# The v stage and the u seam of a hybrid decoder block: shorter roots, diagonals on ScalarE, another order of operands

## The chip, the cores and the metric

The kernel runs on one core of a Trainium2 chip. The metric is the device time of one execution in microseconds (us). TensorE (PE) multiplies, VectorE (DVE) and ScalarE (ACT) do the elementwise work, each in the order of its own queue, and SyncE (SP) issues nearly all DMAs. TensorE's clock is granted by a throttle at one of two levels, 1.2 and 2.4 GHz.

## The reference, cut to what matters

```python
h = rms_norm(x, norm_mix_g[l])                       # x: 1024 tokens x 1024
proj = h @ w_in[l]
rnn_x, rnn_gate, sgu_u, sgu_v, gate_a, gate_b = jnp.split(proj, SPLIT_POINTS, axis=-1)
rnn_x = causal_depthwise_conv(rnn_x, conv_w[l], conv_b[l])
y_a = jax.nn.gelu(rnn_gate) * rg_lru(rnn_x, ..., rg_lambda[l])
y_b = chunked_sgu(jax.nn.gelu(sgu_u), jax.nn.gelu(sgu_v), ...)
# chunked_sgu: v = layer_norm(v); in chunks of 128 tokens mixed = tril(w_s) @ v + b_s; u * mixed
merged = sigmoid(gate_a) * (y_a @ w_proj_a[l]) + sigmoid(gate_b) * (y_b @ w_proj_b[l])
x = x + merged @ w_out[l]
x = x + swiglu(rms_norm(x, norm_ffn_g[l]))           # d_ff 2816
return rms_norm(x, norm_final_g)
# in rg_lru: log_a = -8 * r * softplus(-rg_lambda)
```

## The kernel before

Every matrix product is made of three passes in reduced fp32: an operand is kept as a high part and a low part, and high by high, high by low and low by high are summed (`mm3`, L96 to L99). `split` (L92 to L94) makes the parts: ACT copies the high part, DVE subtracts it for the low one. Most projections are Strassen-Winograd products of 2 x 2 blocks (`wino`, L231): seven products M1 to M7 of blocks and sums of blocks (A11, A12, A22 and the sums S1 to S4 of the activations; b11 to b22 and the sums t1 to t4 of the weights), each with 4 x 3 matmuls of 128 x 512. The weight parts of a product are made by `weight` and `pump` when the product is written, or `state["ahead"]` products earlier.

The program starts with the v stage (pool `phv`, L458 to L785). Its order on each engine is that of the code. x comes in transposed in four blocks (`xt_load`), is scaled and split (`x_split`), and multiplied with the two halves of the v weights, wv0 and wv1, in eight tiles of 128 tokens each (`pv0`, `pv1`). 1/rms of the tokens (`x_rms`) is computed from x in rows by `rstd_early`, a Newton iteration on DVE on one or two columns, and is spread over the free axis by a matmul of ones with a diagonal matrix (`x_diag`, tiles `dg`). A LayerNorm over v (`v_stats`, `v_norm`, `v_centre`; roots for two tiles at once where possible) gives `vn` (`v_split`), which `v_mix` multiplies with the causal 128 x 128 mix weights into PSUM tiles `mx`; ACT and DVE add their two parts into `mt` (`v_mixed`), and SP stores these to the DRAM buffers `mix_d`. Between the tiles of pv1 the operands A11, S1 to S3 and so on are computed from the scaled x (`part`, `sums`, `sum_s4`), because PE needs them right behind.

Then the two u projections, `u0` and `u1`, run product by product in the order M1, M2, M5, M6, M3, M7, M4, with the last two mixes between them (the seam, L752 to L785). Their results wait in PSUM (`postponed`), and `take(n)` takes n of them out. At the end of the seam the pool `phv` is closed and `phr` opened in its place, where `u_out` (L835) loads the mix from `mix_d`, applies the LayerNorm scale and shift (L847), the gelu (L848) and the product (L850) and stores the branch. The recurrence's constants (softplus of lambda, tiles `sp_*`, L873 to L891) and copies of A22 (L866) stand there too. From r0 on, pairs of r, u and g projections follow, then the output projections, the SwiGLU and the last norm, none of which the change edits.

ACT's functions are kept in tables; a function of another table costs an `ACT_TABLE_LOAD` on ACT.

Of the kernel before, what the change touches and what calls it, by code (L numbers as in the profile page):

```python
# [28 lines left out]
RG_C = 8.0  # L29

# [21 lines left out]
def block_kernel(ctx: ExitStack, tc: tile.TileContext, a: dict, out: bass.AP):  # L52
# [323 lines left out]
    act.activation(small.tile([P, 1], F32, name="warm", bufs=1), eps_t, AF.Gelu_apprx_tanh)  # L376
# [16 lines left out]
    def rstd_early(pool_, var, scale, name, n=1, y=None):  # L393
# [5 lines left out]
        dve.tensor_scalar(h, var, -0.5 * scale, -0.5 * EPS, ALU.mult, ALU.add)  # L399
        dve.tensor_scalar(y.bitcast(I32), h.bitcast(I32), -0.5, float(0x5F3759DF - 2 ** 22 - 2 ** 30),  # L400
                          ALU.mult, ALU.add)
        for _ in range(3):
# [5 lines left out]
            dve.scalar_tensor_tensor(y, t, 1.5, y, ALU.add, ALU.mult)  # L408
# [49 lines left out]
    with tc.tile_pool(name="phv", bufs=1) as wk:  # L458
# [88 lines left out]
        def sums(i):  # L547
            s1 = s1s[i] = wk.tile([P, 2, HALF], F32, name=f"xs{i}", tag="shift")
            dve.tensor_add(s1, block(1, 0, i), block(1, 1, i))
            dve.tensor_sub(block(1, 0, i), block(0, 0, i), block(1, 0, i))  # L550
            dve.tensor_sub(block(0, 0, i), s1, block(0, 0, i))
# [13 lines left out]
        ms.__enter__()  # L565
        act.dma_start(pv, a["pv"])
# [10 lines left out]
        state["load"] = 2  # L577
        xt_load(1)
# [7 lines left out]
        for k in range(NK):  # L586
            pump(k + 1)
            x_split(0, (k,))
        acc = {t: ps(f"pv0{t}") for t in range(2)}

        warm = ps("warm")
        for _ in range(8):
# [885 lines left out]
```

## Time and profile before

| | us |
|---|---|
| median of 3 runs (1416.86 to 1420.11) | 1417.53 |
| the profiled execution, whole | 1417.34 |
| its span on the core | 1415.5 |
| PE busy in the span | 1396.2 (99%) |
| DVE busy | 1100.9 (78%) |
| ACT busy | 792.6 (56%) |

The span is the time from the first to the last recorded instruction of the core. PE's busy time counts a matmul at either clock alike, and successive matmuls overlap, so a loss is also looked for in the distance from one start to the next. Times in the rows are counted from the span's start.

### The profile page before, as it was taken

The numbers are of one execution on the slowest core, as the hardware profiler recorded it, in microseconds if no ns is written. First come the engines' busy times: TensorE is split into PE (matmuls) and PEld (weight loads), VectorE is DVE, ScalarE is ACT, GpSimd is POOL, SyncE is SP. The second block draws the span as 40 slices with busy tenths as digits, with TensorE's granted clock in tenths as the row PEclk, the third lists the DMA queues.
The fourth block names the chain that finished last, engine by engine and source line by source line (L and its number), as shares of the span: only waits on it lengthen the run. The fifth ranks groups of instructions, "written<-read, shape, count | busy, mean of one in ns | idle before, by whom it ended". The sixth has DMA issues, their size and how long they took to land.

```text
span 1415.5 us, 17195 instructions
## 1 busy us (share of the span) xinstructions
PE 1396.2 (99%) x6220; PEld 1152.2 (81%) x6220; DVE 1100.9 (78%) x1807; ACT 792.6 (56%) x1318; POOL 75.0 (5%) x59
## 2 busy tenths in 40 slices
PE   9998999999999999999999999999999999999997
PEld 7887887788788888888888788888888888888886
DVE  6999999988888879798756976666666664697586
ACT  8467688888889865443443543333333333444464
POOL 0000000000000000000000021111111111000000
PEclk9999999999999999999999999999999999999999
DMA  9323645433332388774611132232232226842342
GB/s 320 142 60 118 206 153 178 167 113 116 115 110 103 105 306 318 259 297 149 223 60 45 75 112 112 112 112 100 94 112 112 112 84 259 338 179 93 112 142 82
DMA packets 70566, 212.46 MB, mean 150 GB/s; under 512 B 6352, under 2 KB 20176, under 8 KB 57936
## 3 DMA queue, kind: packets, MB, share of 16 engines
q1 hardware_dynamic: 70192, 211.05, 41.7%
q8 instruction: 49, 0.80, 0.2%
q10 hardware_dynamic: 288, 0.30, 0.1%
q14 instruction: 37, 0.30, 0.1%
HBM read 148.68 MB, written 62.65 MB: 149 GB/s over the span
## 4 chain that ended last, share of the span: by engine, by line
PE 76%; DVE 12%; ACT 8%; issue 2%; DMA 1%; SPq 0%; DVEq 0%; ACTq 0%
PE f_p L97 10%; PE f_p L99 10%; PE f_p L98 10%; PE d_M L98 5%; PE d_M L99 5%; PE d_M L97 5%; PE g_p L99 2%; PE g_p L98 2%; PE g_p L97 2%; PE pa_p L99 2%; PE pa_p L98 2%; PE pb_p L99 2%; PE pb_p L98 2%; PE pa_p L97 2%; PE pb_p L97 2%
## 5 line engine op out<-in xcount | busy, mean ns | idle before, releaser
L93 ACT ACTIVATE dl_M<-wraw 128x512 fp32r<-128x512 f32 x77 | 48.6, 631 | 104.2 <-PE d_M L99 94.3
L93 ACT ACTIVATE f_t<-wraw 128x512 fp32r<-128x512 f32 x88 | 55.2, 630 | 84.3 <-PE f_p L99 64.1
L98 PE MATMUL d_M<-d_M,dl_M 128*128 128x512 f32 x260 | 101.2, 389 | 0.0
L97 PE MATMUL d_M<-d_M,dl_M 128*128 128x512 f32 x260 | 101.2, 389 | 0.0
L99 PE MATMUL d_M<-d_M,dl_M 128*128 128x512 f32 x260 | 101.1, 389 | 0.0
L94 DVE TENSOR_TENSOR dl_M<-wraw,dl_M 128x512 fp32r<-128x512 f32 x77 | 54.0, 701 | 49.5 <-ACT dl_M L93 49.3
L94 DVE TENSOR_TENSOR f_t<-wraw,f_t 128x512 fp32r<-128x512 f32 x88 | 70.8, 806 | 23.1 <-ACT f_t L93 22.1
L97 PE MATMUL f_p<-f_S,f_t 128*128 128x512 f32 x176 | 68.6, 390 | 0.3 <-ACT f_t L93 0.3
L97 PE MATMUL f_p<-m,f_b 128*128 128x512 f32 x176 | 68.6, 390 | 0.0
L98 PE MATMUL f_p<-f_S,f_t 128*128 128x512 f32 x176 | 68.5, 389 | 0.0
L99 PE MATMUL f_p<-m,f_b 128*128 128x512 f32 x176 | 68.5, 389 | 0.0
L98 PE MATMUL f_p<-m,f_t 128*128 128x512 f32 x176 | 68.5, 389 | 0.0
L99 PE MATMUL f_p<-m,f_t 128*128 128x512 f32 x176 | 68.5, 389 | 0.0
L98 PE MATMUL f_p<-m,f_b 128*128 128x512 f32 x176 | 68.5, 389 | 0.0
L99 PE MATMUL f_p<-f_S,f_t 128*128 128x512 f32 x176 | 68.4, 390 | 0.0
L97 PE MATMUL f_p<-m,f_t 128*128 128x512 f32 x176 | 68.3, 389 | 0.0
L94 DVE TENSOR_TENSOR f_b<-wraw,f_b 128x512 fp32r<-128x512 f32 x66 | 47.2, 718 | 15.6 <-ACT f_b L93 14.9
L93 ACT ACTIVATE f_b<-wraw 128x512 fp32r<-128x512 f32 x66 | 40.9, 625 | 32.5 <-PE f_p L99 29.9
L98 PEld LDWEIGHTS d_M<-d_M,dl_M 128*128 128x128 f32 x260 | 48.8, 188 | 10.4 <-DVE d_M L94 0.2
L97 PEld LDWEIGHTS d_M<-d_M,dl_M 128*128 128x128 f32 x260 | 48.8, 188 | 10.2
L99 PEld LDWEIGHTS d_M<-d_M,dl_M 128*128 128x128 f32 x260 | 48.8, 188 | 10.0
L197 DVE TENSOR_TENSOR wraw<-wraw 128x512 f32<-128x512 f32 x50 | 53.0, 1060 | 1.1
(524 smaller groups left out, 4219.8 us busy)
## 6 DMA issues: line engine op xcount, KB each, us to landing
wraw<-in_w_gu_dram SPq DMA_DIRECT2D x22, 1024.0 KB, 5.0
wd<-in_w_down_dram SPq DMA_DIRECT2D x11, 1024.0 KB, 8.9
wraw<-in_w_r_dram SPq DMA_DIRECT2D x8, 1024.0 KB, 6.7
wraw<-in_w_g_dram SPq DMA_DIRECT2D x8, 1024.0 KB, 4.9
wraw<-ffs_d SPq DMA_DIRECT2D x8, 1024.0 KB, 5.1
wraw<-ffa_d SPq DMA_DIRECT2D x6, 1024.0 KB, 5.9
xn<-in_x_dram SPq DMA_DIRECT2D x8, 512.0 KB, 9.0
wraw<-in_w_u_dram SPq DMA_DIRECT2D x4, 1024.0 KB, 5.5
```

Source lines behind the costliest of these rows:

```text
L93: act.activation(hi, src, AF.Copy)
L94: return (eng or dve).tensor_sub(lo, src, hi.bitcast(F32))
L97: pe.matmul(o, lh, rh, start=start, stop=False, **kw)
L98: pe.matmul(o, lh, rl, start=False, stop=False, **kw)
L99: pe.matmul(o, ll, rh, start=False, stop=stop, **kw)
L197: dve.tensor_sub(raw[:, 0], raw[:, 2], raw[:, 0])
```

## The change

- `rstd_early`: one Newton step and one step of third order in place of three Newton steps: 9 steps on DVE for 11 with two columns, 7 for 8 with one.
- `x_diag`: 1/rms is split into high and low part first (two columns), and ACT makes the four diagonals; DVE made two of them.
- `sums(i)` is taken apart into `sum_s1`, `sum_s3`, `sum_s2`, and these and the parts are given to other tiles t of pv1.
- Mixes: `mix_out` joins two `mt` tiles into one and stores them with one DMA; the splits of the next `vn` and the adds stand per half.
- The seam calls for weight sums and weight parts by name between the products (`state["ahead"] = 0`), S4's second sum stands behind M6, and the operands S4, S3 and A22 and the copies of A22 are written inside the seam, the latter in `phr`'s tiles.
- The recurrence's constants move to the front of the program, with the table load for their Exp; lambda is loaded at the start.
- x's first piece is issued by ACT's queue ahead of `pv`, SP issues the others; 10 warm-up matmul calls in place of 8 (two instructions each).

```diff
@@ rstd_early @@
-        for _ in range(3):
+        def product():
             if n == 1:
                 dve.scalar_tensor_tensor(t, y, y, h, ALU.mult, ALU.mult)
             else:
                 dve.tensor_mul(t, y, y)
                 dve.tensor_mul(t, t, h)
-            dve.scalar_tensor_tensor(y, t, 1.5, y, ALU.add, ALU.mult)
+        dve.tensor_scalar(h, var, -scale / 4.5, -EPS / 4.5, ALU.mult, ALU.add)
+        dve.tensor_scalar(y.bitcast(I32), h.bitcast(I32), -0.5, ROOT_BITS, ALU.mult, ALU.add)
+        product()
+        dve.scalar_tensor_tensor(y, t, 1.5, y, ALU.add, ALU.mult)
+        product()
+        dve.scalar_tensor_tensor(t, t, 5.0 / 3.0, t, ALU.add, ALU.mult)
+        dve.scalar_tensor_tensor(y, t, 1.25, y, ALU.add, ALU.mult)
@@ x_diag @@
+            split(hi, lo, rms[:, c])
             dg = dgs[q] = wk.tile([P, 2, 2, P], F32R, name=f"dg{q}", tag="vb", bufs=3)
-            for i in range(2):
-                r = rms[:, 2 * q + i:2 * q + i + 1]
-                act.activation(dg[:, 0, i], ident, AF.Copy, scale=r)
-                dve.scalar_tensor_tensor(dg[:, 1, i], ident, r, dg[:, 0, i].bitcast(F32), ALU.mult, ALU.subtract)
+            for n, r in enumerate((hi.bitcast(F32), lo)):
+                for i in range(2):
+                    act.activation(dg[:, n, i], ident, AF.Copy, scale=r[:, i:i + 1])
@@ the head @@
+        act.activation(table, eps_t, AF.Exp)
+        xt_load(0, slice(0, 1), act)
         act.dma_start(pv, a["pv"])
...
-                if j == 0 and k < 2:
-                    xt_load(0, slice(k, k + 1))
+                if (j, k) == (0, 0):
+                    xt_load(0, slice(1, 2))
...
-        for _ in range(8):
+        for _ in range(10):
             pe.matmul(warm[:, :P], ident, ident, start=True, stop=True, skip_group_check=True)
@@ mixes @@
+        def mix_out(t, q):
...
+            for i in range(2):
+                act.activation(m[:, i], mts[t, 2 * q + i][:, :, 1], AF.Copy)
+            for i in range(2):
+                dve.tensor_add(m[:, i], m[:, i], mts.pop((t, 2 * q + i))[:, :, 0])
+            nc.sync.dma_start(mix_d[q][:, :, ts(t)], m.rearrange("p i j t -> p (i j) t"))
@@ the tiles of pv1 @@
-            if t < 2:
-                scale_x(1, range(4 * t, 4 * t + 4))
-            if 1 <= t < 3:
-                part("A11", block(0, 0, t - 1), t - 1)
+            if t == 0:
+                scale_x(1, range(NK))
+            if t == 1:
+                for i in range(2):
+                    part("A11", block(0, 0, i), i)
+                sum_s1(0)
+                sum_s3(0)
             if t == 2:
-                sums(0)
+                sum_s2(0)
+            if t == 3:
+                sum_s1(1)
+                sum_s3(1)
...
@@ the seam @@
-        state["ahead"] = 3
+        state["ahead"] = 0
...
         v_mix(7)
-        v_mixed(7)
-        part("S2", block(0, 0, 0), 0)
+        for q in range(2):
+            mix_out(7, q)
+        sums13("u1", raw["u1"])
+        pump(where["u1", "M5"] + 1)
         head("u1")
-        part("S2", block(0, 0, 1), 1)
+        for i in range(2):
+            part("S2", block(0, 0, i), i)
+        sum2("u0", raw["u0"])
+        pump(where["u0", "M6"] + 1)
+        head("u0")
+        sum2("u1", raw["u1"])
+        pump(where["u1", "M6"] + 1)
+        head("u1")
+        take(4)
+        sum_s4(1)
+    with tc.tile_pool(name="phr", bufs=2) as wk:
+        for i in range(2):
+            part("S4", block(0, 1, i), i)
+        head("u0")
+        head("u1")
+        for i in range(2):
+            part("S3", block(1, 0, i), i)
         take(2)
         head("u0")
+        a22 = [wk.tile([P, 2, HALF], F32, name=f"a22_{i}", tag="rr") for i in range(2)]
+        for i in range(2):
+            act.activation(a22[i], block(1, 1, i), AF.Copy)
+        state["ahead"] = 3
         head("u1")
```

ACT's queue at the start of the program, before (tile `x` is transposed x, `h` its scaled parts, `wv_0` the first v weight part):

```order
L566 DMA pv<-in_pv_dram 128x80
L376 ACT_TABLE_LOAD
L376 ACTIVATE warm<-eps_t 128x1
L585 ACTIVATE ones<-ident 128x128
L93 ACTIVATE wv_0_175<-wraw_152 128x512
L483 ACTIVATE h_131<-x_129,pv 128x256
```

and in the change:

```order
L614 ACT_TABLE_LOAD
L614 ACTIVATE table<-eps_t 128x1
L499 DMA x_129<-in_xt_dram 128x256
L617 DMA pv<-in_pv_dram 128x80
L628 DMA lam<-in_lam_dram 128x8
L636 ACTIVATE ones<-ident 128x128
L94 ACTIVATE wv_0_178<-wraw_155 128x512
L509 ACTIVATE h_131<-x_129,pv 128x256
```

The DMA of x now stands on this queue, behind the table load and its activation, and pv's behind both.

DVE's queue in the seam before, from u1's b22 part (`u_b_1427`) to its M6 part (`u_t_1431`) and the operands of M3 and M7 (`h_S_1460`, `u_t_1481`); L847 and L850 are steps of the gate branch on the loaded `mix`:

```order
L94 TENSOR_TENSOR u_b_1427<-wraw_646,u_b_1427 128x512
L847 SCALAR_TENSOR_TENSOR mix_1505<-mix_1505,pv,sh_1508 128x512
L204 TENSOR_TENSOR wraw_646<-wraw_646 128x512
L850 TENSOR_TENSOR u_y_1342<-mix_1505,u_y_1342 128x512
L847 SCALAR_TENSOR_TENSOR mix_1514<-mix_1514,pv,sh_1517 128x512
L226 TENSOR_TENSOR wraw_646<-wraw_646 128x512
L850 TENSOR_TENSOR u_y_1344<-mix_1514,u_y_1344 128x512
L94 TENSOR_TENSOR u_t_1431<-wraw_646,u_t_1431 128x512
L94 TENSOR_TENSOR h_S_1460<-x_129,h_S_1460 128x2x512
L847 SCALAR_TENSOR_TENSOR mix_1565<-mix_1565,pv,sh_1508 128x512
L94 TENSOR_TENSOR h_S_1460<-x_129,h_S_1460 128x2x512
L94 TENSOR_TENSOR u_t_1481<-wraw_620,u_t_1481 128x512
```

and in the change, from u0's b22 part (`u_b_1418`) on; `u_t_1422` and `u_t_1442` are the M6 parts of u0 and u1, L945 is the former L847:

```order
L95 TENSOR_TENSOR u_b_1418<-wraw_656,u_b_1418 128x512
L205 TENSOR_TENSOR wraw_656<-wraw_656 128x512
L945 SCALAR_TENSOR_TENSOR mix_1555<-mix_1555,pv,sh_1558 128x512
L95 TENSOR_TENSOR u_t_1422<-wraw_656,u_t_1422 128x512
L95 TENSOR_TENSOR u_b_1438<-wraw_682,u_b_1438 128x512
L945 SCALAR_TENSOR_TENSOR mix_1564<-mix_1564,pv,sh_1567 128x512
L205 TENSOR_TENSOR wraw_682<-wraw_682 128x512
L945 SCALAR_TENSOR_TENSOR mix_1573<-mix_1573,pv,sh_1558 128x512
L945 SCALAR_TENSOR_TENSOR mix_1579<-mix_1579,pv,sh_1567 128x512
L95 TENSOR_TENSOR u_t_1442<-wraw_682,u_t_1442 128x512
L246 TENSOR_TENSOR u_y_1341<-u_y_1341,u_p_1345 128x512
L246 TENSOR_TENSOR u_y_1343<-u_y_1343,u_p_1400 128x512
```

The first step on a loaded `mix` has moved ahead of u0's M6 part, and three more ahead of u1's. In before two stood ahead of u1's part, and none ahead of u0's.

DVE's queue in the change further on, up to the M7 parts of u0 and u1 (`u_t_1523`, `u_t_1526`); L600 is S4's second sum and `h_S_1498` is S3:

```order
L600 TENSOR_TENSOR x_129<-x_129 128x1024
L95 TENSOR_TENSOR h_S_1469<-x_129,h_S_1469 128x2x512
L948 TENSOR_TENSOR u_y_1341<-mix_1555,u_y_1341 128x512
L95 TENSOR_TENSOR h_S_1469<-x_129,h_S_1469 128x2x512
L948 TENSOR_TENSOR u_y_1343<-mix_1564,u_y_1343 128x512
L227 TENSOR_TENSOR wraw_682<-wraw_682 128x512
L95 TENSOR_TENSOR h_S_1498<-x_130,h_S_1498 128x2x512 x2
L254 TENSOR_TENSOR u_u_1503<-u_u_1503,u_p_1425 128x512
L254 TENSOR_TENSOR u_u_1505<-u_u_1505,u_p_1445 128x512
L945 SCALAR_TENSOR_TENSOR mix_1612<-mix_1612,pv,sh_1558 128x512
L945 SCALAR_TENSOR_TENSOR mix_1641<-mix_1641,pv,sh_1567 128x512
L95 TENSOR_TENSOR u_t_1523<-wraw_656,u_t_1523 128x512
```

In before the M7 part of u0 stood directly behind S4's second half; now S3's two halves and four steps of the results stand between.

## Rows read from the trace of the kernel before

**Rows 1.** The page's first part: busy time, share of span, instructions by engine.

```profile
PE 1396.2 (99%) x6220; PEld 1152.2 (81%) x6220; DVE 1100.9 (78%) x1807; ACT 792.6 (56%) x1318; POOL 75.0 (5%) x59
```

**Rows 2.** Waits of PE over the span: releaser, us in total, times, longest.

```profile
PE u_p L97 <- ACT u_t L93: 2.5, 1, 2.5
PE mx L696 <- DVE vn L684: 1.9, 3, 1.2
PE mx L695 <- ACT vn L683: 1.2, 1, 1.2
```

**Rows 3.** Window 140 to 150 us: busy time by engine, granted clock, DMA share.

```profile
140.00:150.00 10.00, 9.81 (x36) 7.65 (x37) 8.63 (x12) 8.76 (x13) 0.00 (x0) 0.83 0.25 75
```

**Rows 4.** Timeline of PE at 78 us: start, us, instruction, idle before, releaser.

```profile
78.07 0.39 PE L98 MATMUL pv<-wv,h 128*128 128x512 f32 x1
78.30 0.39 PE L99 MATMUL pv<-wv,h 128*128 128x512 f32 x1
79.93 0.38 PE L695 MATMUL mx<-ws,vn 128*128 128x256 f32 x1 [1.25 <-ACT vn L683]
```

**Rows 5.** Timeline of DVE at the second LayerNorm root of the v stage.

```profile
76.58 0.16 DVE L399 TENSOR_SCALAR rv<-mv 128x2 f32<-128x2 f32 x1
78.63 0.74 DVE L704 TENSOR_TENSOR mt<-mt,mx 128x256 f32<-128x256 f32 x2
```

**Rows 6.** Timeline of DVE at 50 us: a diagonal, and the wv1 splits.

```profile
50.05 0.64 DVE L500 SCALAR_TENSOR_TENSOR dg<-ident,rms,dg 128x128 fp32r<-128x128 f32 x2 [0.55 <-ACT dg L499]
54.19 2.48 DVE L94 TENSOR_TENSOR wv<-wraw,wv 128x512 fp32r<-128x512 f32 x4
```

**Rows 7.** Timelines of DVE, ACT and PE at the seam, 125 to 161 us.

```profile
125.40 1.78 DVE L704 TENSOR_TENSOR mt<-mt,mx 128x256 f32<-128x256 f32 x4
133.34 1.23 DVE L94 TENSOR_TENSOR h_S<-x,h_S 128x1024 fp32r<-128x1024 f32 x1 [0.26 <-ACT h_S L93]
134.49 1.28 DVE L245 TENSOR_TENSOR u_y<-u_y,u_p 128x512 f32<-128x512 f32 x2
143.81 0.69 DVE L94 TENSOR_TENSOR u_t<-wraw,u_t 128x512 fp32r<-128x512 f32 x1
...
130.78 1.06 ACT L866 ACTIVATE a<-x 128x1024 f32<-128x1024 f32 x1 [2.59 <-DMA mix_d<-mt]
137.75 1.28 ACT L879 ACT_TABLE_LOAD   x1
139.16 0.61 ACT L93 ACTIVATE u_t<-wraw 128x512 fp32r<-128x512 f32 x1
...
139.83 0.50 PE L97 MATMUL u_p<-h_S,u_t 128*128 128x512 f32 x1 [2.55 <-ACT u_t L93]
...
161.01 0.39 PE L97 MATMUL r_p<-h_A,r_b 128*128 128x512 f32 x1
```

**Rows 8.** DMA issues of single windows: count, KB, us to landing (last: page).

```profile
mix_d<-mt SPq DMA_DIRECT2D x1, 128.0 KB, 1.9
mix_d<-mt SPq DMA_DIRECT2D x1, 128.0 KB, 3.3
mix<-mix_d SPq DMA_DIRECT2D x1, 256.0 KB, 2.8
...
wraw<-in_w_r_dram SPq DMA_DIRECT2D x8, 1024.0 KB, 6.7
```

**Rows 9.** The head: timelines of ACT and PE, and pv's DMA.

```profile
0.81 0.40 ACTq L566 DMA_DIRECT2D pv<-in_pv_dram  x1
6.29 0.51 ACT L483 ACTIVATE h<-x,pv 128x256 fp32r<-128x256 f32 x1 [1.08 <-DMA x<-in_xt_dram]
...
6.85 0.80 PE L97 MATMUL pv<-wv,h 128*128 128x512 f32 x1 [1.64 <-ACT h L483]
10.86 0.44 PE L97 MATMUL pv<-wv,h 128*128 128x512 f32 x1
...
pv<-in_pv_dram ACTq DMA_DIRECT2D x1, 40.0 KB, 3.9
```

More of the change, by code (lines that the diff above doesn't have):

```diff
@@ L29 @@
 RG_C = 8.0
+ROOT_BITS = float(0x5F3759DF - 2 ** 22 - 2 ** 30)
 PV = {}
@@ L545, in block, with sum_s1, sum_s3, sum_s2 @@
             return F[h][:, 4 * kh + 2 * i:4 * kh + 2 * i + 2]
[L547 to L551 removed]
+        def sum_s1(i):
+            if i == 0:
+                s1s[i] = [wk.tile([P, 2, HALF], F32, name="xs0", tag="shift")]
+            else:
+                s1s[i] = [wk.tile([P, HALF], F32, name=f"xs1{k}", tag="va", bufs=8).rearrange("p (k t) -> p k t", k=1)
+                          for k in range(2)]
+            for k, s1 in enumerate(s1s[i]):
+                c = slice(k, k + s1.shape[1])
+                dve.tensor_add(s1, block(1, 0, i)[:, c], block(1, 1, i)[:, c])
+        def sum_s3(i):
+            dve.tensor_sub(block(1, 0, i), block(0, 0, i), block(1, 0, i))
+        def sum_s2(i):
+            for k, s1 in enumerate(s1s[i]):
+                d = block(0, 0, i)[:, k:k + s1.shape[1]]
+                dve.tensor_sub(d, s1, d)
+        def part_s1(i):
+            for k, s1 in enumerate(s1s[i]):
+                part("S1", s1, i, k)
         def sum_s4(i):
@@ L565, in block_kernel @@
         ms.__enter__()
+        table = small.tile([P, 1], F32, name="table", bufs=1)
+        act.activation(table, eps_t, AF.Exp)
+        xt_load(0, slice(0, 1), act)
         act.dma_start(pv, a["pv"])
@@ L733, in block_kernel @@
                 v_norm(t)
-            if t > 1:
+            if 1 < t < NT - 1:
                 v_mix(t - 2)
-                v_mixed(t - 2)
+                for q in range(2):
+                    mix_out(t - 2, q)
             if t == group[t][-1]:
@@ L750, in block_kernel @@
         U = {n: wino(n, ops, *(call(n, i) for i in range(4)), order=LATE) for n in ("u0", "u1")}
-        state["ahead"] = 3
+        raw = {n: loads[queue[where[(n, "M1")]][0]][2] for n in U}
+        state["ahead"] = 0
         def head(n):
@@ L762, in block_kernel @@
         cur["defer"] = True
-        v_split(6)
         head("u0")
+        pump(where["u0", "M2"] + 1)
         v_mix(6)
-        v_mixed(6)
-        v_split(7)
+        for q in range(2):
+            v_split(7, q)
+            mix_out(6, q)
+        pump(where["u1", "M2"] + 1)
         head("u1")
@@ L770, in block_kernel @@
         head("u0")
+        sums13("u0", raw["u0"])
+        pump(where["u0", "M5"] + 1)
         v_mix(7)
-        v_mixed(7)
-        part("S2", block(0, 0, 0), 0)
+        for q in range(2):
+            mix_out(7, q)
+        sums13("u1", raw["u1"])
+        pump(where["u1", "M5"] + 1)
         head("u1")
-        part("S2", block(0, 0, 1), 1)
+        for i in range(2):
[15 more added lines that the diff above has]
+            part("S3", block(1, 0, i), i)
         take(2)
         head("u0")
+        a22 = [wk.tile([P, 2, HALF], F32, name=f"a22_{i}", tag="rr") for i in range(2)]
+        for i in range(2):
+            act.activation(a22[i], block(1, 1, i), AF.Copy)
+        state["ahead"] = 3
         head("u1")
-        part("S4", block(0, 1, 0), 0)
-        take(2)
-        part("S4", block(0, 1, 1), 1)
-        head("u0")
-        head("u1")
-        take(2)
+        for i in range(2):
+            part("A22", a22[i], i)
         cur["defer"] = False
-    ms.__exit__(None, None, None)
-    with tc.tile_pool(name="phr", bufs=2) as wk:
+        ms.__exit__(None, None, None)
+        for fn in postponed:
+            fn()
+        postponed.clear()
         shifts = {}
```

120 lines of the change are left out of this document (58 added, 62 removed).

## The prediction

> **What bounds the kernel now.** I read the page's engine line first: TensorE (PE) is busy for 1396.2 of the span's 1415.5 us [rows 1], so all that an edit outside the matmuls can win is 19.3 us of idle time plus whatever the lower of TensorE's two clocks costs. Second, PE's waits: the largest are 2.5 us for a u weight part from ScalarE (ACT), 1.9 and 1.2 us for the normalised v operand `vn` from VectorE (DVE) and ACT [rows 2]. All lie before 140 us, where the change works. Third, the windows: from 140 to 150 us the granted clock is 0.83 and PE is busy all the same [rows 3]; so the 2.5 us wait is followed by matmuls at the 1.2 GHz level, a loss that no list of waits shows. Fourth, the timeline of the engine each wait names, back to what held it.
>
> The stall at 79.93 us: PE issues its last pv1 matmul at 78.30 and the second mix's first matmul at 79.93 [rows 4]. `vn` needs the LayerNorm root, which DVE computes from 76.58 to 78.63 in 11 small steps 0.2 us apart, and then four adds of the mix before ACT's and DVE's parts of `vn` [rows 5]. DVE does not wait in this stretch; it is simply behind, and the same backlog gives the waits near 110 and 116 us.
>
> The stall at 139.83 us has another cause. ACT stands in order: the copy of A22 at 130.78 waits 2.59 us for stores of the mix to leave memory it is to take, then a table load of 1.28 us comes in, and the u weight split is only reached at 139.16 [rows 7]. Behind it the window's 0.83 of the clock means 1.7 us of the ten lost by lower speed; in the head, matmuls at that level start 0.445 us apart (9 from 6.85 to 10.86 [rows 9]) and 0.23 at the full clock (78.07 to 78.30 [rows 4]).
>
> **The change, priced.** All sums are against the profiled execution of 1417.34 us, which agrees with the median 1417.53 to 0.02%.
>
> *Roots and diagonals.* A two-column root loses 2 of 11 steps at 0.2 us, 0.4 us [rows 5]; a one-column root one step. Seven pairs stand on DVE (four for x, three for v) and two singles: 3.2 us. In each of the four diagonals DVE drops two 128x128 steps (0.64 us a pair, behind a wait of 0.55 in two of them) for one tiny one: about 0.45 x 4 + 0.55 x 2 = 2.9 us [rows 6]. ACT gets two more diagonal copies and a tiny one, some 0.8 us each time, at places where it waited for that root. The 16 steps of the recurrence's constants, 3.2 us at the same 0.2, move ahead of the first x root, where DVE waits for ACT's sums of squares; there are 25 us in which what is left over can be absorbed. So DVE reaches the wv1 splits (54.19 [rows 6]) up to 1.6 + 2.9 = 4.5 us sooner. They cannot all come that much sooner, since each takes the place of a wv0 part that PE still reads; I take 3.2 us. With 0.2 for the next root and 0.4 for its own steps, the root that ended at 78.63 is done near 74.8, and `vn`, some 1.3 us of adds behind it, near 76.1: in time for PE at 78. The waits for `vn`, 3.1 us [rows 2], go, and a few tenths at the first wv1 matmul; PE's restarts cost more than the wait (79.93 is 1.63 us after 78.30 at a pace of 0.23, for a wait of 1.25 [rows 4]), so I put the v stage at **-4.3 us**, between -2.5 (waits near 116 stay: adding up DVE's steps at these prices leaves it under 1 us of slack there, an estimate) and -5.
>
> *The seam.* What comes next is limited by DVE. The last add of the last mix ends at 127.18 in before (125.40 + 1.78) [rows 7] and follows PE, so now near 122.9. The order shows what DVE has from there to the second part of u0's M7 weight, without a gap to choose: 23 steps of 512 columns at 0.63 us from start to start and 7 of 1024 columns at 1.15 (1.28 for two of the one kind at 134.49; 1.23 for one of the other at 133.34, the next 1.15 after it [rows 7]): 14.5 + 8.0 = 22.5 us. PE has from the end of that mix only u1's M2, two M5, two M6 and two M3 (7 x 12 x 0.227 = 19.1 us), and then starts M7. In before u0's M7 part ended at 144.5 (143.81 + 0.69 [rows 7]), 17.3 us after the last add, waits and all; the change puts S3, S4's second sum and more of the gate branch's steps ahead of it, as the order of DVE's queue shows. One of these steps, the first on `mix`, needs a round trip through DRAM that starts with the last add: a store of 1.9 to 3.3 us, then a load of 2.8 and the small shift load behind it [rows 8], with issue 5.5 to 7 us; DVE has 5.7 us of other work before it, so it waits 0 to 1.4 us, and u0's and u1's M6 weights wait behind it. I take 0.7. u0's M7, held at its third pass, then goes on at 122.9 + 22.5 + 0.7 = 146.1; 20 matmuls of M7 and 24 of M4 follow (10.0 us), with about 0.5 us for the A22 parts: r0 starts near 156.6, and did at 161.01 [rows 7]. That is **-4.4 us including the v stage**: the cause of the 139.83 stall goes, but some 3 us of waits come back at M6, M3 and M7.
>
> *The head.* x's first piece moves to the front of ACT's queue, behind a table load; pv stands behind it. In before PE's first real matmul is at 6.85, released by ACT's scaling at 6.29, which waited for x [rows 9]. If ACT issues past the table load (about 1.0 us), x lands near 4.9 and pv 0.4 later (pv took 3.9 from its issue at 0.81 [rows 9]), and ACT and PE follow 0.55 us behind. The 20 warm matmuls end later than that: 16 ended 1.64 us before 6.85, at 5.2, so 20 near 6.2. First matmul: 6.2. If it issues only behind the load and its activation (0.81 + 1.28 + 0.2 = 2.3, the load's price from [rows 7]), x lands at 6.2, pv at 6.6, and the first matmul comes at 7.2. So -0.65 to +0.35. With less idle before it, the full clock, which came at 10.86 after 9 matmuls 0.445 us apart [rows 9], may come sooner, worth up to 9 x 0.215 = 1.9 us. I take **-1.0**, between +0.4 and -2.5. A rule speaks against this edit: the Trainium skill, "DMA: Bandwidth & Descriptors", section "Issuing engines are not separate DMA queues", says that transfers of all issuing engines share the same 16 engines, and that another issuer saves only issue time. By that rule alone the head would win one issue slot, some 0.5 us.
>
> *Tables.* One pair of loads, 1.28 us each [rows 7], leaves the seam; ACT is not the last there any more, so I price it at nothing (cover: DVE's list). The Trainium skill, "ScalarE: Activation LUTs", section "What ACT_TABLE_LOAD costs", counts 2.66 us a switch with its drain; here the weight split starts 1.41 us after the load at 137.75 does, with a small activation between [rows 7], so no drain of that size shows. *Mix stores, 16 for 32:* only SP's issue time. *Constants out of the r stage:* 3.2 us less on DVE near 170 us, a few tenths at most: -0.3, between -1.5 and +1.
>
> Sum: -4.4 - 1.0 - 0.3 = -5.7; 1417.3 - 5.7 = **1411.6 us**.
>
> **The rivals.** *Full gain:* DVE's list is shorter than I count, or PE's M3 and M7 do not meet it; then all losses of the stretch go, 4.3, at the seam 4.6 (2.55 and about 2 for the clock [rows 3, 7]) and 1.5 at the head: 10.4, or 1407. For it: DVE's idle time ahead of M7 in before goes to work now, and a list of 30 steps is only as good as its prices. Against: 5% off a list of 22.5 us is 1.1 us, and 3 are wanted.
>
> *The clock falls again:* the wait at M7 is about 2 us, and a wait of 2.55 us was what stood before the fall at 139.83, while one of 1.25 us was not followed by a fall [rows 4, 7]. Price 2 us: 1413.6. The Trainium skill, "TensorE: Matmul & The Clock Gate", Part 1, has idle time lower the clock; the row at 139.83 agrees.
>
> *The v stage stays late:* DVE has under 1 us of slack at the mixes 1, 5 and 6; if the wv1 splits gain 1.5 us and not 3.2, the waits near 80 and 116 us keep about 2.5 us: 1414.1.
>
> *Slower than before:* the r0 weights. Their 1 MB load is now issued behind the stores of u's first results, near 148.9, 7.7 us ahead of r0; in before r0's load went out 10 us ahead. Such a load takes 6.7 us in the median [rows 8] and its splits 1.2, so it is on the edge. Each us over that is 1:1; from 5.7 us over, that is a landing of over 12 us, or the same lateness given on to the r and u pairs that follow, it decides: 1419.
>
> **Chances.** My forecast 0.45, full gain 0.22, clock 0.13, v stage late 0.12, slower 0.08. The measurement tells a change from none at about 0.2%, 2.8 us: faster is below 1414.7. Forecast, full gain, most of the clock case and half of the late v stage are faster: 0.79; same 0.14; slower 0.07. The range goes from 1405.0 (full gain with a full head) to 1415.6 (late v stage with a late head).
>
> **What would show it.** PE's wait at 79.93 is gone and the root behind it ends near 75 us; the x piece on ACT's queue is issued near 1.0 (or 2.3); DVE shows a wait for a mix load of under 1.4 us, and PE's largest wait in the seam is for a u weight part at M7, 1.5 to 2.5 us, for DVE or ACT; clock 1.00 there. r0 starts near 155.5 (156.6 less the head). It is wrong if r0 starts before 152 or after 158, or if the difference lies behind 165 us.

## The result and the profile after

The changed kernel took **1429.29 us** (median of 4 runs, 1428.20 to 1431.02) against 1418.40 for the kernel before on the same chip (4 runs, 1416.86 to 1420.11): a ratio of 1.0082, 95% interval 1.0068 to 1.0095. It is slower by 0.8%; 1411.6 was forecast. The profiled execution took 1428.2 us, its span is 1426.4, 10.9 more than before. Where PE stood at four points of the program, by the start of its matmuls:

| PE starts | before | after | difference |
|---|---|---|---|
| the first diagonal, behind pv0's first four tiles | 30.65 | 29.82 | -0.8 |
| pv1, first tile | 54.33 | 61.21 | +6.9 |
| u0's M5 (the first u product that needs a sum) | 128.96 | 135.45 | +6.5 |
| r0 | 161.01 | 171.06 | +10.05 |

So two stretches lose: 30 to 61 us, and the seam. Between them the new wait at the first mix stands against waits of before that are gone. What lies behind r0 differs by 0.9 us. These are single profiles: the twelve kernels of this document that have the head of after, itself among them, have the first diagonal at 29.56 to 30.83, and the five kernels D0 to D4, alike up to the seam, have u0's M5 at 126.87 to 128.15. The -0.8 is within this spread of 1.3 us.

The page's first part, and PE's waits up to 230 us (releaser, us in total, times, longest), both of after:

```profile
PE 1401.2 (98%) x6224; PEld 1153.5 (81%) x6224; DVE 1096.7 (77%) x1790; ACT 793.7 (56%) x1331; POOL 75.0 (5%) x59
```

```profile
PE mx L751 <- DVE vn L739: 2.7, 1, 2.7
PE u_p L100 <- DVE u_t L95: 1.9, 3, 1.1
PE rs L557 <- ACT ws L94: 1.8, 1, 1.8
PE rs L558 <- DVE ws L95: 1.8, 1, 1.8
PE u_p L98 <- ACT u_t L94: 1.5, 2, 1.3
...
PE r_p L98 <- ACT r_t L94: 1.1, 1, 1.1
```

Against [rows 2] the list is longer, and the waits on `ws` and `r_t` are new. DVE has 4.2 us less to do than in [rows 1] (1096.7 for 1100.9), and PE has more idle time: the change took work from DVE and yet made PE wait for it.

**The diagonals.** ACT's timeline of after, from the first diagonal on (start, us, instruction, idle before and releaser):

```profile
27.16 0.70 ACT L529 ACTIVATE dg<-ident,rh 128x128 fp32r<-128x128 f32 x2
30.14 0.69 ACT L529 ACTIVATE dg<-ident,rl 128x128 fp32r<-128x128 f32 x2 [2.29 <-DVE rl L95]
...
35.87 0.20 ACT L94 ACTIVATE rh<-rms 128x2 fp32r<-128x2 f32 x1 [1.81 <-DVE rms L434]
37.30 3.29 ACT L509 ACTIVATE h<-x,pv 128x256 fp32r<-128x256 f32 x8
45.63 0.21 ACT L94 ACTIVATE rh<-rms 128x2 fp32r<-128x2 f32 x1 [1.81 <-DVE rms L434]
49.71 1.04 ACT L94 ACTIVATE ws<-ws_raw 128x1024 fp32r<-128x1024 f32 x1
54.71 0.20 ACT L94 ACTIVATE rh<-rms 128x2 fp32r<-128x2 f32 x1 [3.96 <-DVE rms L434]
57.27 1.15 ACT L94 ACTIVATE wv<-wraw 128x512 fp32r<-128x512 f32 x2
```

and DVE's of the same stretch:

```profile
26.78 3.26 DVE L510 SCALAR_TENSOR_TENSOR h<-x,pv,h 128x256 fp32r<-128x256 f32 x8
29.96 0.15 DVE L95 TENSOR_TENSOR rl<-rms,rh 128x2 f32<-128x2 f32 x1
37.82 3.29 DVE L510 SCALAR_TENSOR_TENSOR h<-x,pv,h 128x256 fp32r<-128x256 f32 x8 [1.55 <-ACT h L509]
60.10 3.08 DVE L95 TENSOR_TENSOR wv<-wraw,wv 128x512 fp32r<-128x512 f32 x5
```

The low diagonals need `rl`, a subtraction of 0.15 us on DVE that stands behind eight subtractions of `x_split(2)`; ACT waits 2.29 us for it. The second diagonal now stands ahead of `x_split(3)`, and so ACT waits for the root (1.81) with eight scalings queued behind that wait; they start at 37.30. Each later diagonal meets the root late again. In before ACT waited for the root too, but at two of the four diagonals only:

```profile
ACT dg L499 <- DVE rms L408: 9.0, 2, 5.9
```

In after its waits for `rms` and `rl` add up to 9.9 us, hardly more, but they begin at the first diagonal, ahead of work that DVE needs: between 20 and 62 us DVE waits 8.2 us for ACT, in before 3.1. The two engines take turns in waiting for each other. DVE reaches the wv1 splits at 60.10, 5.9 us later than in [rows 6], and PE stands at `rs`, which the late `ws` holds:

```profile
50.80 0.50 PE L557 MATMUL rs<-ws,ones 128*128 128x512 f32 x1 [1.81 <-ACT ws L94]
53.08 0.51 PE L558 MATMUL rs<-ws,ones 128*128 128x512 f32 x1 [1.77 <-DVE ws L95]
```

**The first mix.** DVE's timeline of after, then PE's:

```profile
74.24 2.36 DVE L95 TENSOR_TENSOR h_A<-x,h_A 128x1024 fp32r<-128x1024 f32 x2 [1.01 <-ACT h_A L94]
76.52 1.22 DVE L585 TENSOR_TENSOR xs<-x 128x1024 f32<-128x1024 f32 x1
77.77 1.23 DVE L588 TENSOR_TENSOR x<-x,x 128x1024 f32<-128x1024 f32 x1
79.76 0.70 DVE L739 SCALAR_TENSOR_TENSOR vn<-va,rv,vn 128x512 fp32r<-128x512 f32 x1
...
80.51 0.33 PE L751 MATMUL mx<-ws,vn 128*128 128x128 f32 x1 [2.69 <-DVE vn L739]
```

The root of this mix was done at 73.2; between it and `vn` stand both halves of A11, S1 and S3. In before one half of A11 and four scalings of x stood there, and the two sums came behind `vn` (69.47); the new tile order put the second half and the sums ahead. The wait moved from the second mix [rows 4] to the first.

**The clock** behind these two places and in the seam: windows of after (sum, busy time by engine, granted clock, DMA share):

```profile
40.00:60.00 20.00, 16.41 (x65) 13.03 (x64) 15.72 (x45) 14.16 (x32) 1.18 (x1) 0.91 0.28 116
80.00:100.00 20.00, 19.49 (x102) 17.23 (x103) 16.42 (x43) 12.34 (x25) 0.00 (x0) 0.91 0.18 53
160.00:180.00 20.00, 18.91 (x76) 14.66 (x76) 16.22 (x25) 9.93 (x16) 0.00 (x0) 0.93 0.77 243
```

and the first two of before:

```profile
40.00:60.00 20.00, 19.80 (x89) 16.15 (x88) 18.88 (x45) 10.26 (x20) 0.00 (x0) 1.00 0.25 89
80.00:100.00 20.00, 19.56 (x108) 16.87 (x109) 18.96 (x42) 15.39 (x30) 0.00 (x0) 1.00 0.27 79
```

A granted clock of 0.91 means some 1.8 us (20 x 0.09) lost to the 1.2 GHz level in each of the two, and 0.93 some 1.4, which no list of waits shows.

**The seam.** DVE and PE of after:

```profile
133.22 1.41 DVE L763 TENSOR_TENSOR mt<-mt,mx 128x256 f32<-128x256 f32 x4
141.72 0.75 DVE L945 SCALAR_TENSOR_TENSOR mix<-mix,pv,sh 128x512 f32<-128x512 f32 x1 [1.16 <-DMA mix<-mix_d]
158.43 1.29 DVE L95 TENSOR_TENSOR u_t<-wraw,u_t 128x512 fp32r<-128x512 f32 x2
...
143.13 0.50 PE L100 MATMUL u_p<-h_S,u_t 128*128 128x512 f32 x1 [1.11 <-DVE u_t L95]
157.66 0.50 PE L98 MATMUL u_p<-h_S,u_t 128*128 128x512 f32 x1 [1.26 <-ACT u_t L94]
159.18 0.74 PE L100 MATMUL u_p<-h_S,u_t 128*128 128x512 f32 x1 [0.27 <-DVE u_t L95]
```

Here the forecast order of events is there: the stall of 2.55 at 139.83 [rows 7] is gone, DVE waits for the mix load, M6 and M7 wait. u0's M7 part ends 24.5 us after the last mix add (134.6 to 159.1); 23.2 was forecast. From u0's M5 to r0 it is 35.6 us, in before 32.05; from the last mix add to r0 36.4, in before 33.8.

### The profile page after: what moved, and what is told of

It reads as the page before. It is cut to its first block, busy times and chain, and to the rows that moved or that the text cites. A ratio compares the mean times of both kernels' runs of the same rounds, so it can differ in the third digit from the quotient of the medians.

```text
span 1426.4 us, 17134 instructions
## 1 busy us (share of the span) xinstructions
PE 1401.2 (98%) x6224; PEld 1153.5 (81%) x6224; DVE 1096.7 (77%) x1790; ACT 793.7 (56%) x1331; POOL 75.0 (5%) x59
## 4 chain that ended last, share of the span: by engine, by line
PE 73%; DVE 14%; ACT 9%; issue 2%; DMA 2%; SPq 0%; DVEq 0%; ACTq 0%; POOL 0%; POOLq 0%
PE f_p L100 9%; PE f_p L99 9%; PE f_p L98 9%; PE d_M L98 5%; PE d_M L100 5%; PE d_M L99 5%; PE g_p L99 2%; PE g_p L100 2%; PE g_p L98 2%; PE pa_p L98 2%; PE pb_p L99 2%; PE pb_p L98 2%; PE pa_p L100 2%; PE pa_p L99 2%; PE pb_p L100 2%
```

## Experiments

Ratios are to the kernel before on the same chip, with 95% intervals.

| kernel | us | ratio |
|---|---|---|
| after | 1429.29 | 1.0082 (1.0068 to 1.0095) |
| A1 diagonals back | 1425.47 | 1.0051 (1.0034 to 1.0068) |
| A2 head back | 1432.62 | 1.0103 (1.0088 to 1.0118) |
| A3 tile order back | 1425.36 | 1.0053 (1.0038 to 1.0068) |
| A4 seam back | 1422.64 | 1.0032 (1.0020 to 1.0044) |
| B1 = A1 + A3 + A4 | 1414.69 | 0.9968 (0.9958 to 0.9978) |
| B2 = B1, x by SP | 1414.26 | 0.9966 (0.9954 to 0.9978) |
| B3 = B2, lambda by POOL | 1414.63 | 0.9970 (0.9959 to 0.9982) |
| B4 = B3, constants late | 1414.94 | 0.9972 (0.9961 to 0.9982) |
| C before + roots + warm-up | 1414.84 | 0.9973 (0.9963 to 0.9983) |
| D0 = A1 + A3, new seam | 1420.67 | 1.0012 (1.0003 to 1.0021) |
| D1 = D0, mix steps last | 1426.36 | 1.0062 (1.0049 to 1.0075) |
| D2 = D0, M7's weights first | 1419.15 | 1.0005 (0.9996 to 1.0014) |
| D3 = D1 + D2 + M4's weights | 1428.15 | 1.0069 (1.0057 to 1.0081) |
| D4 = D2, mix steps behind A22 | 1423.95 | 1.0035 (1.0021 to 1.0049) |

The main theory was that each of three parts loses on its own (diagonals, tile order, seam). The rival was one chain: the v stage gets late in one place and the rest only passes that on.

### A1 to A4: one part undone

A1, the diagonals and their place:

```diff
-            split(hi, lo, rms[:, c])
...
+                act.activation(dg[:, 0, i], ident, AF.Copy, scale=r)
+                dve.scalar_tensor_tensor(dg[:, 1, i], ident, r, dg[:, 0, i].bitcast(F32), ALU.mult, ALU.subtract)
...
-                x_diag(1)
                 x_split(3)
+                x_diag(1)
```

> The changed kernel (1429.3 us) with the diagonals as before: DVE makes the low ones, and x_diag(1) stands behind x_split(3) again. Theory A, diagonals: PE's wait for the mix weights near 51 us comes from ACT, which waits for DVE's two-column low part (2.3 us behind eight subtractions) and for roots that no x_split covers any more (1.8 us twice). Then ACT reaches the wv1 splits near 53 us and not at 57.3, PE's two waits of 1.8 us there go with the 1.3 us of low clock behind them and 1.7 us at the rms matmuls: about 6 us less, 1423. Rival, the head: the lateness is that of the loads (second x block landed 18.13 us, 16.55 before); then these waits stay at 2 us or more and the time falls by at most 1.5, to 1428.

A2, the head (x, lambda, the constants' place):

```diff
-        xt_load(0, slice(0, 1), act)
-        act.dma_start(lam, a["lam"])
-        recurrence_constants(wk)
...
         run(U["u0"], U["u1"])
+        load(lam, a["lam"])
+        recurrence_constants(wk)
```

> The changed kernel with the head's DMAs as before (x by SP, pv alone on ACT's queue) and with lambda's load, the constants and their table loads back behind the seam; 10 warm-up calls stay. Theory B, head: lambda's load and x and pv on ACT take places among the outstanding DMAs, so SP issues later and the second x block lands 1.6 us later; undone, everything up to the wv1 splits comes about 1.6 us sooner: 1.5 to 2 us less, 1427.5, and PE still waits about 2 us near 51 us. If the head were the whole cause, 5 us or more would go: 1424. If ACT's and DVE's order alone sets that stretch, nothing: 1429.

A3, the tile order of pv1:

```diff
-            if t == 0:
-                scale_x(1, range(NK))
-            if t == 1:
-                for i in range(2):
-                    part("A11", block(0, 0, i), i)
+            if t < 2:
+                scale_x(1, range(4 * t, 4 * t + 4))
+            if 1 <= t < 3:
+                part("A11", block(0, 0, t - 1), t - 1)
+            if t == 2:
                 sum_s1(0)
                 sum_s3(0)
```

> The changed kernel with the scaling of x, the sums and the parts A11, S1 and A12(0) at the tiles t of pv1 where they stood before. Theory C, tiles: the wait of 2.85 us at 80.5 for the first mix's vn and the 1.5 us of low clock behind it come from A11's two halves and two sums, 4.7 us of DVE, that now stand ahead of that vn. Then this wait goes, but the second mix's wait (2 us in the kernel before) comes back: 2 to 4 us less, 1426.5. Rival: DVE is late there because the wv1 splits are 5.9 us late, wherever the sums stand; then less than 1 us changes.

A4 has the seam, its pool boundary and the last tile's operands as before (`state["ahead"] = 3`, S3 and A22 behind the gate branch); `mix_out` stays.

> The changed kernel with the last tile of the v stage and the seam in the order before, phr opened behind it, S3, A22 and the copies of A22 behind the results. Theory D, seam: from u0's M5 to r0 the changed kernel takes 35.6 us and the kernel before 32.05, by waits at M6, M3 and M7 and a fall of the clock at M7; undone, the 3.5 us go: 1425.8. Rival: the seam only takes over lateness of the v stage; then less than 1 us changes.

Measured against after: A1 -3.8 us, where about 6 were expected, A3 -3.9, A4 -6.7, where 3.5 were. A1 takes PE's waits for `ws` away and puts pv1's first tile at 55.59 for 61.21; its wait at the first mix stays. A3 is the other way round. These are the waits of PE in A1, then in A3:

```profile
PE mx L748 <- DVE vn L736: 3.1, 1, 3.1
```

```profile
PE rs L557 <- ACT ws L94: 1.8, 1, 1.8
PE rs L558 <- DVE ws L95: 1.8, 1, 1.8
...
PE mx L751 <- DVE vn L739: 0.4, 1, 0.4
```

A2 says nothing on the head: moved back, lambda's two activations came with two table loads at 29 to 33 us, in the middle of the v stage, so it has a cost that neither kernel has.

### The diagonals taken apart

Two kernels with only one half of A1's edit, run once each: the four diagonals on ACT but behind `x_split(3)`, and the low ones on DVE but ahead of it.

```diff
-                x_diag(1)
                 x_split(3)
+                x_diag(1)
```

> The changed kernel with x_diag(1) behind x_split(3) again, the diagonals all on ACT. If the place of x_diag(1) ahead of x_split(3) is what exposes the roots on ACT, ACT starts the wv1 splits 3 us or more sooner than 57.3 us. If it is the low part on DVE, which stands behind x_split's subtractions, ACT only waits for that at the second diagonal too (2 us or more), and wv1 starts within 1 us of 57.3.

```diff
-            split(hi, lo, rms[:, c])
...
+                dve.scalar_tensor_tensor(dg[:, 1, i], ident, r, dg[:, 0, i].bitcast(F32), ALU.mult, ALU.subtract)
```

> The changed kernel with the low diagonals on DVE again, x_diag(1) left ahead of x_split(3). If the wait for the two-column low part is the cause, wv1 starts near 54 us; if the place is, ACT still waits 1.8 us for each root, x_split(3) stands behind it, and wv1 starts at 55.5 us or later.

ACT's first wv1 split is at 57.27 in after, 56.76 in the first, 54.10 in the second and 52.56 in A1. The place alone gives 0.5 us, the engine alone 3.2, both 4.7; the spans, 1429.1 and 1425.5, are of one profile each, and D0 to D4, with this stretch alike, have the split at 51.39 to 52.94. PE's first pv1 tile is at 61.21, 59.80, 58.71 and 55.59. So the engine is the larger part; the place adds to it (58.71 to 55.59), and by itself it is too small to tell from that spread. What costs is that ACT, in order, waits for a small result of DVE that has longer work ahead of it.

### B1 to B4 and C: what is left, and what gains

B1 is after with A1, A3 and A4 together.

> The changed kernel with the diagonals, the tiles of pv1 and the seam as before, all three. What stays of the change: short roots, constants and lambda's load in front, x and pv on ACT's queue, 10 warm-up calls, mixes stored per half. If the losses found one by one add up, 1429.3 - 3.8 - 3.9 - 6.7 = 1414.9, that is 2.5 to 3.5 us faster than the kernel before; wv1 starts at 54 us or sooner and no wait over 1 us stands between 20 and 75 us. Rival: they share one lateness, so that undoing one already takes part of the others' gain; then the sum is 5 to 8 us in place of 14 and it ends near 1422, slower than before.

1414.69: the three losses add up (3.8 + 3.9 + 6.7 = 14.4; 1429.29 - 14.4 = 1414.9), so the rival chain falls, and what is left of the change beats both kernels by 0.3%. B2 to B4 ask what in that rest is of use:

```diff
-        xt_load(0, slice(0, 1), act)
...
+                if j == 0 and k < 2:
+                    xt_load(0, slice(k, k + 1))
```

> The same with x's first piece issued by SP again and pv first on ACT's queue (lambda stays behind pv on ACT). Theory B: x and pv on ACT change the order in which SP's issues find a place; with them back, the second x block lands near 17.3 us and not 18.2, and the time falls by 0.5 to 1 us against the kernel beside it. Rival: what counts is lambda's load, which takes one more place; then x's issuer changes nothing (within 0.5 us).

```diff
-        act.dma_start(lam, a["lam"])
+        nc.gpsimd.dma_start(lam, a["lam"])
```

> The kernel with diagonals, tiles, seam and x's issuer as before (1414.3 us), with lambda's load moved from ACT's queue to POOL's. Theory B, places: lambda's 4 KB took one of the places among the DMAs that are under way in the head, so that SP issued the later pieces one landing later; with it gone from there the second x block lands near 17 us and not 18.8, PE's waits at the rms matmuls (1.1 us) go, and the time falls by 1 to 1.5: 1413. Rival: the landings are paced by what all transfers move, and lambda's 128 short rows cost the same on any queue: no change.

```diff
-        recurrence_constants(wk)
         x_rms(0)
...
+                if f == 0:
+                    recurrence_constants(wk)
```

> The kernel of the run beside it, with the 16 DVE steps of the constants called for by the first gate pair (they then stand in DVE's waits of the seam), while lambda's Abs and Exp stay in the head. If the 3.2 us of DVE steps ahead of the first x root delay the rms matmuls, these come sooner and up to 1 us more goes: 1412.5. If DVE is not what holds them, or the seam has no room for the steps, the time is the same or up to 1 us more.

All three are within 0.4 us of B1: neither x's issuer nor the place of lambda's load nor that of the 16 DVE steps is worth anything that shows in the time. C is the kernel before with two edits alone, the short roots and ten warm-up calls:

```diff
-        for _ in range(3):
+        product()
+        dve.scalar_tensor_tensor(y, t, 1.5, y, ALU.add, ALU.mult)
+        product()
+        dve.scalar_tensor_tensor(t, t, 5.0 / 3.0, t, ALU.add, ALU.mult)
+        dve.scalar_tensor_tensor(y, t, 1.25, y, ALU.add, ALU.mult)
...
-        for _ in range(8):
+        for _ in range(10):
```

> The kernel before with the short roots and 10 warm-up calls alone. If the gain of the three-times undone kernel (4.1 us) comes from the constants' leaving the seam (lambda's wait of 1.1 us and a table load of 1.28 us on ACT ahead of u1's M6 part, and the low clock behind), this one keeps the seam's waits and gains only what the roots give in the v stage and the clock in the head, 1 to 2 us: 1416.5. If the roots and the warm-up are the gain, 1414.5.

C is as fast as B1, by another way. Its time is the one expected if the roots and the warm-up were the gain, and yet B1 gains elsewhere: in C u0's M5 starts at 126.67 (before 128.96) and the seam keeps its stall; in B1 u0's M5 is at 129.39 and the old seam has lost its stall, 29.1 us to r0 for 32.05. PE's row in C, and its waits in B1's seam:

```profile
138.14 0.80 PE L98 MATMUL u_p<-h_S,u_t 128*128 128x512 f32 x1 [3.14 <-ACT u_t L94]
```

```profile
PE u_p L98 <- ACT u_t L94: 0.9, 1, 0.9
```

In before and in C ACT waits for lambda and runs the table load ahead of this u part (137.75 and 139.16 [rows 7]). In B1 both are gone from there and the part starts at 137.94, behind a wait of 1.23 us for DVE; the copy of A22 ahead of it still waits 2.43 us for the mix stores. B4, with the 16 DVE steps late and lambda's activations in front, has 0.6 us at that place, so it is not the DVE steps.

### D0 to D4: inside the seam

D0 is after with A1 and A3, so that the new seam stands alone.

> The changed kernel with diagonals and tiles as before, the new seam kept. Theory D: the new seam costs by its own order (DVE's list ahead of M7, the mix load, r0's late weights), whatever came before it: 1414.7 + 6.7, about 1421. Rival: it only took over lateness of the v stage; then 1415 to 1417.

6.0 us more than B1. u0's M5 starts 2.5 us sooner than in B1 (126.87), and r0 3.0 later (161.51); the rest lies behind r0. Three waits are there: M6 behind DVE's wait for the mix load, M7 behind ACT's copies of A22, and an `r_t` part. Are they single waits in a row (theory A), or is DVE's work up to r0 the bound, so that each only takes the place of another (theory B)? D1 puts the mix steps behind all operands, D2 writes M7's weights first, D3 does both.

```diff
+        pump(where["u1", "M7"] + 1)
         take(2)
         head("u0")
...
-        ms.__exit__(None, None, None)
         for fn in postponed:
             fn()
...
         for fn in results:
             fn()
         results.clear()
+        ms.__exit__(None, None, None)
```

The first + line is D2, the last and the - line are D1; D3 has "M4" for "M7".

> The change with its old diagonals and old tile order (the kernel that took 1420.67 us), and besides it the gate branch's steps on the loaded mix (the norm's scale and shift, the gelu, the product) stand behind the operands of u's last products on DVE and ACT, not between them. Theory A (in the new seam these steps are what holds u0's M6 weight: DVE waits 1.92 us there for a load of mix, PE 2.04 and then 8 matmuls at the lower clock level, 1.6): the loss of 3.6 us goes and M7's 1.4 stays, since ACT's copies of A22 still stand ahead of its weights: 1417.0. Theory B (DVE's list is too long as such, and the wait only takes the place of a later one): M6 starts on time, but M3 or M7 waits by as much more: 1419.5 to 1421. If the four steps moved behind hold up the r stage's first weights instead, r0 waits and the time is 1420 or more.

> The same kernel (1420.67 us) with the weight parts of u0's and u1's M7 written directly behind S3, ahead of ACT's copies of A22 and of the results that are taken out. Theory A (M7 waits because of what stands ahead of its weights on ACT and DVE): PE's waits of 1.42 and 0.43 at M7 go, 1.6 us, and the wait at M6 stays: 1419.0. Theory B (S3 itself comes too late, so the weights only wait for their turn): no change, 1420.7.

> Both of these edits, and M4's weight parts written behind M7's, so that the buffer of u0's raw weights comes free sooner and the load for r0 is issued some 3 us sooner. Theory A: the three waits at M6, M7 and r0 (3.6, 1.6 and 1.3 us) go: 1414.2; since the first u product that needs a sum starts 2.5 us sooner here than in the best kernel so far (126.87 against 129.39), r0 may start before 156 us, and then the time is under 1414, down to 1412. Theory B (DVE's work up to M7 is the bound): the waits merge into one before M7 or r0, 1417 to 1420.

In D2 M7's wait is gone (0.2 us is left), as theory A says, but r0's first part now waits 0.9; the medians differ by 1.5 us, the ratios by 1.0, and their intervals overlap. D1 did as theory A says up to r0: M7 starts 19.4 us after u0's M5 (D0 22.8), r0 30.55 after it (D0 34.6). But then PE stands for 9.5 us, a fall of the clock with it, and the time rises by 5.7:

```profile
175.90 0.79 PE L98 MATMUL r_p<-h_S,r_t 128*128 128x512 f32 x1 [9.46 <-ACT r_y L243]
```

ACT's copy `r_y` waits there for a store of the branch: its result takes a tile that the gate branch holds until its rows are stored, and these now come last. D3 has the same wait, 6.9 us, and one of 4.1 before M7; its 1428.15 lies outside both theories. D4 looks for a place between the two: the mix is loaded early, the steps stand directly behind A22's parts.

```diff
+        for q in range(2):
+            mixes[q, 0, 0] = mix_load(q, 0, 0)
...
         for i in range(2):
             part("A22", a22[i], i)
+        for q in range(2):
+            res[f"u{q}"] = u_outs(q)
+        for fn in results:
+            fn()
         ms.__exit__(None, None, None)
```

> The seam with M7's weights first (1419.15 us), and the mix steps behind A22's parts as in the run that took 1426.36, but with the four loads of mix issued at the start of the stretch, and with the results of M3 taken out ahead of M7's weights' second part as there they were not: so that the first rows of the branch are stored, and their tiles free, some 10 us sooner than in that run, where the r stage's first copy waited 9.5 us for such a tile. Theory A (waits in a row: the mix load ahead of M6, 3.6 us, the copies of A22 ahead of M7, 1.5, and behind them whatever holds r0): no wait above 1 us up to r0, r0 near 156.5, no wait for a tile behind it: 1415. If the tiles still come late, a wait in the r stage of 2 to 5 us: 1417 to 1420. Theory B (DVE's list is the bound): r0 is not before 160 and the time 1419 or more.

r0 is at 157.14, as theory A forecast (156.5), 29.0 us after u0's M5 and as good as B1; but r0's own second part is then waited for 1.4 us and a part of the next r product 3.4, behind the steps that were moved. What lies behind r0 takes 9.8 us longer than in B1, and the time is 1423.95 for the 1415 of theory A. PE's waits in D4:

```profile
PE r_p L98 <- ACT r_b L94: 3.4, 1, 3.4
...
PE r_p L100 <- DVE r_b L95: 1.4, 1, 1.4
```

The windows 125 to 185 us of B1, D0, D1, D4 and C, in this order of the fences (columns as above; DVE's busy time is the third with a count):

```profile
125.00:185.00 60.00, 58.62 (x265) 48.14 (x264) 56.65 (x87) 39.99 (x65) 0.20 (x2) 1.00 0.54 175
```

```profile
125.00:185.00 60.00, 55.06 (x225) 42.39 (x224) 53.63 (x81) 34.18 (x55) 0.10 (x1) 0.97 0.55 176
```

```profile
125.00:185.00 60.00, 47.91 (x196) 37.20 (x195) 50.77 (x74) 31.22 (x50) 0.10 (x1) 0.91 0.43 143
```

```profile
125.00:185.00 60.00, 53.74 (x219) 41.82 (x219) 52.01 (x77) 31.48 (x52) 0.10 (x1) 0.94 0.50 162
```

```profile
125.00:185.00 60.00, 56.86 (x238) 46.39 (x238) 54.70 (x95) 39.23 (x62) 0.20 (x2) 0.94 0.52 173
```

In B1 DVE is busy for 56.65 of these 60 us; 3.4 us are left in it, and 8 to 16 steps of 0.7 us were moved. Among the kernels with the new seam and B1, the more DVE stands idle (3.4, 6.4, 9.2 and 8.0 us), the longer the kernel (1414.7, 1420.7, 1426.4, 1424.0), in the same order; D2 and D3 fit in (5.0 and 12.4 us; 1419.2 and 1428.2). C does not: 5.3 us idle, and 1414.8. So neither theory holds as put: the waits are single ones, each goes when its cause goes, but the steps moved out of the way are wanted soon after. That DVE's idle time is the cause and not a companion of PE's is argued, since DVE also waits for PE there (2.5 us in D4), and not shown.

## Why the prediction was wrong

The last mix add, put near 122.9, ended at 134.6, and at 127.2 in before: the v stage's term came out at +7.4 us for -4.3, mostly by the two steps named first here; with both undone (D0) that add ends at 126.0. From there to r0 2.7 us more were lost than forecast. The sign has no single cause: with any one part undone the kernel stays slower than before (A1, A3, A4), and with the first two undone as well (D0).

**"Roots and diagonals" failed.** The step booked DVE's savings (3.2 us in the roots, 2.9 in the diagonals) and let ACT's added work stand "at places where it waited for that root". That holds for two of the four diagonals in before; at the first two ACT did not wait. The step priced the copies, and not the wait that came with them: the change gave ACT a dependence on DVE in the middle of its queue, twice (`rms`, then `rl`), with eight scalings behind it. The wv1 splits came 5.9 us later instead of 3.2 sooner. With the diagonals back (A1) DVE reaches them at 55.38, still 1.2 later than before, and in C at 52.39, 1.8 sooner: up to 3.0 us go with the new front (B1 55.37), which the step did not book; with lambda issued by POOL it is 53.75 (B3), in one profile each. The short roots do gain: alone with the warm-up they bring 0.27% (C, 3.8 us). In C's profile the warm-up has hardly a part in that: nine starts behind the first real matmul are still 0.42 to 0.60 apart, and the first diagonal is 0.15 us sooner than before; the other executions are not told apart. At C's second mix PE waits 0.4 us, for 1.25 and 0.44.

**"vn near 76.1, some 1.3 us of adds behind the root" failed as well.** The step took before's order [rows 5] for the second mix and put nothing on the first, though the diff put A11's second half, S1 and S3 ahead of the first mix's `vn`: 6.5 us from the root's end at 73.2 to 79.76, where before had 4.5 (64.94 to 69.47). The second mix's `vn` came at 87.29. A3 prices the tile order at 3.9 us.

**"The seam" had the mechanism and mis-sized it.** The list of DVE, the wait for a mix load (1.16 for 0.7), the wait at M7 for a u part, and the fall of the clock behind it (the rival "the clock falls again") all came. The stretch from the last add to r0 was put at 33.7 us, 0.1 less than before, and took 36.4: 1.3 more from the list and the wait, the rest at M7 and behind. The worse error is one of credit: the new order was to pay for its own waits with the end of the 139.83 stall. B1 has the old order with the constants at the front, and that stall is all but gone there too. Against that, the new order costs 6.0 us (D0 against B1).

**"Tables: nothing" failed for that reason too.** ACT was the last there in before, with lambda's wait and the table load, and the cover that I named (DVE's list) was that of the new seam.

**"The head"** was forecast at -1.0; at 30 us -0.8 is left, within the spread of single profiles. x was issued at 0.97, as forecast, past the table load that runs from 0.80 to 2.08; but it landed 4.7 us after its issue and pv, which the first scaling waited for last, 5.1 us after its own, and the first matmul came at 7.17 for 6.2:

```profile
0.80 1.28 ACT L614 ACT_TABLE_LOAD   x1 [0.80 <-PEq L1539]
0.97 0.38 ACTq L499 DMA_DIRECT2D x<-in_xt_dram  x1
6.61 0.51 ACT L509 ACTIVATE h<-x,pv 128x256 fp32r<-128x256 f32 x1 [1.23 <-DMA pv<-in_pv_dram]
...
x<-in_xt_dram ACTq DMA_DIRECT2D x1, 128.0 KB, 4.7
pv<-in_pv_dram ACTq DMA_DIRECT2D x1, 40.0 KB, 5.1
...
7.17 0.50 PE L98 MATMUL pv<-wv,h 128*128 128x512 f32 x1 [1.24 <-ACT h L509]
```

pv took 5.1 us for the 3.9 of [rows 9]. In this profile the clock came sooner: after 7.17 the next starts are 0.34 and 0.23 apart, where before had nine at 0.445. That is not a sure gain: with the same head A1 and A3 have six and eight starts at 0.42 to 0.59 behind the first matmul. The rule cited against this edit (the Trainium skill, "DMA: Bandwidth & Descriptors", section "Issuing engines are not separate DMA queues") agrees with B1 against B2: issued by ACT or by SP, the kernel takes 1414.69 or 1414.26 us.

**The slower rival** (r0's weights late) was there with 1.1 us at `r_t` in after, far from deciding anything. No rival named ACT waiting for DVE in the v stage, and the range ended at 1415.6. Its low end, 1405.0, is not the sum of its terms either (1407 less 1.0 for a full head is 1406); nothing hangs on that.

Left open: which of the waits in D0 makes how much of its 6.0 us (D2 changes too little to price M7's); and whether C's time at u0's M5 and B1's seam can be had together, which was not tried. u0's M5 is later than in C by 2.7, 2.8, 1.1 and 2.2 us in B1 to B4, but only by 0.2 in D0, which has the constants at the front as well; so they need not cost it, and what does is not shown.

## What to carry to other kernels

Work moved to an engine that is idle is free only if it can start when its turn comes: look at what the idle engine waits for, and at what is queued behind the moved instruction, before its busy time is counted. When one diff has several parts, price each against the old order of all the others, or one part is given the credit for what another does; here the end of a stall was booked to the new order, which the old order has too once lambda's load and the table load are out of the way. In a stretch where one engine is busy for 94% of the time (56.65 of 60 us), the new orders tried here (D0 to D4) moved the waits, and all stayed slower than the old one: ask of each step that is put back who wants its result, and whose tile it holds.

## What the runs showed that was not expected

- A DMA on ACT's queue is issued while the table load of the same engine runs: issue at 0.97, load from 0.80 to 2.08.
- The clock behind the warm-up is not the same in each execution: in after the wait of 1.24 us ahead of the first real matmul is not followed by the lower level, in A3 one of 1.15 is, and in D3 one of 1.59 is not, all with the same head. The wait of 2.69 at 80.51 is followed by it (0.91 over the 20 us from 80).
- lambda's 4 KB on ACT's queue took 5.5 us to land, and the second block of x landed at 18.13 us for 16.55 in before (17.9 to 19.0 in D0 to D4); with lambda issued by POOL it was 17.41, and PE's warm-up then began 1 us later, since the same engine makes its operand. The time was the same in each case.
